# An RWKV7 mixer rearranged: decay on the state, key-query products among the projections, joined inverses in two wide tiles

## The chip, the cores and the metric

The kernel runs on one core of a Trainium2 chip. The metric is the device time of one execution in microseconds. The time before is 3166.21 us, the median of three runs (3164.11 to 3168.96).

TensorE (PE) does matmuls and transposes, VectorE (DVE) elementwise work and 32x32 block transposes, ScalarE (ACT) activations and copies, GpSimd (POOL) elementwise work and fills; the SyncE queue (SP) issues the loads of weights.

## The reference, cut to what matters

The program is a transformer of six layers in fp32. The last four are blocks of FFN, mixer, FFN; the mixer of the first and the last of these is an RWKV7 time mix (16 heads of 64, 256 tokens). It is this:

```
dx = token_shift(h) - h
xr, xw, xk, xv, xa, xg = [h + dx * mu[j] for j in range(6)]
r, k, v = xr @ w_rkv[0], xk @ w_rkv[1], xv @ w_rkv[2]
w = -softplus(-(w0 + tanh(xw @ w1) @ w2)) - 0.5
decay = exp(-exp(w))
a = sigmoid(a0 + (xa @ a1) @ a2)
if vres is None: v_first = v                 # first call
else: v = v + (v_first - v) * sigmoid(v0 + (xv @ v1) @ v2)   # second call
g = sigmoid(xg @ g1) @ g2
kk = normalized heads of k * k_k
k = k * (1 + (a - 1) * k_a)
def step(state, inp):                        # for each token, per head 64x64
    sa = state @ -kk_t
    state = state * w_t + outer(sa, kk_t * a_t) + outer(v_t, k_t)
    return state, state @ r_t
y = group norm of the outputs over each head, * ln_w + ln_b
bonus = sum(r * k * r_k) * v                 # per head and token
out = ((y + bonus) * g) @ w_o
```

## The kernel before, in words

One function, `rwkv(i, j)` (lines 1351 to 1778), does a whole mixer and is called twice: j = 0 near 883 to 1150 us of the profiled span, j = 1 near 2690 to 2945 us. Channels lie on partitions; a tile of 128x512 holds 128 channels twice by 256 tokens, so that the 1024 channels are four such tiles (index w) or eight halves (index k, two heads each). The tokens are cut into four chunks (index c) of 64. Within a chunk the recurrence becomes matrix products and the inverse of a unit triangular 64x64 matrix per head and chunk; between the chunks a state is carried.

A weight matrix of 128x2048 comes from memory into one of three staging slots ("raw", line 334 on); ScalarE rounds it to a high part wH (L341), VectorE subtracts to make the low part wL (L343), and TensorE multiplies with high and low parts (function `mm3`; L320 is the line of every plain matmul). The names of the stages below are mine.

- **A, preparation.** For each w the projection of r runs, and `prep(w)` forms the normalized keys kk, the cumulated decay W and its inverse iW (a scan cs and two exponentials), kw (keys times decay, L1492, and a copy of its first columns, L1493), and the tiles AP and BK. BK holds two halves: L1504 on VectorE, L1505 on GpSimd, which also clears AP. `inter(w)` multiplies AP with BK on TensorE (phb), transposes AP (phe), and leaves masked triangles in L3 (tile lc) and AM.
- **B, inverse by columns.** VectorE transposes L3 in four pieces (L1614), then subtracts column after column in 31 steps (L1621, L1623) and transposes the result twice (L1626 and L1627, tile tdt). Two inverses of 32x32 stand for each 64x64 triangle. Between the column steps `late()` issues other work in portions: the mixes and low-rank products for g and v (l1b, l1c), the v projection, in the second call the gate sv and the mixing of v with the first layer's v (vf, L1406 to L1408), and the second low-rank product of g (matmuls ps<-g,raw).
- **C, `reads()`.** For each w: the product r times k times r_k (L1575) summed by a matmul (bs), r times decay (L1577), the key-query products pha of TensorE with 64 rows, their masks PA (L1586), bh = BK times the decay at a chunk's end (L1591, half on GpSimd), its transposes pt, kept as BKT, and the bonus tiles.
- **D, joining.** The 32x32 inverses become 64x64 ones: products pn and px of 32x32 matrices, copies into block tiles BD (64 on ScalarE, 32 on VectorE, each 32x128), and GT = AM times BD (matmul pg).
- **E, the chunks.** For each c: `values` (pv), `solve` (pu, then two copies into sv), `advance` (matmul pst with BKT, the new state), `read` (py), the norm, and `back`. The state is pst plus ws, the old state times the decay, which GpSimd makes (L1717).

The order of the work is not the order of the code alone: a scheduler of the framework places the instructions on each engine by priority, and tiles wait for free slots of their pools: three raw slots, three "big" ones, 44 data tiles of 128x512 ("d"), three PSUM tiles "ps", two for transposes, two "otile".

Of the kernel before, what the change touches and what calls it, by code (L numbers as in the profile page):

```python
# [241 lines left out]
class Kern:  # L242
# [1108 lines left out]
    def rwkv(self, i, j):  # L1351
        nc, A = self.nc, self.A
        vres = j > 0
        rb = self.rstd_b()
# [121 lines left out]
        def prep(w):  # L1476
# [17 lines left out]
            for m in range(2):  # L1494
# [10 lines left out]
                nc.gpsimd.tensor_tensor(b4[:, :, 64:128], c4(kt[w], m), c4(iW, m), OP.mult)  # L1505
# [19 lines left out]

        next(rproj)
        prep(0)
        for w in range(4):
            if w < 3:
                prep(w + 1)  # L1530
                next(rproj)
            inter(w)
        GG = BO = None
# [34 lines left out]
        def reads():  # L1568

            for w in range(4):  # L1570
                pb = self.otile("bs")
                for m in range(2):
                    k, sl = 2 * w + m, slice(m * 256, m * 256 + 256)
                    q = self.t2("rk")[:, :256]
                    nc.vector.scalar_tensor_tensor(q, r[w][:, sl], vj("r_k", k), kt[w][:, sl], op0=OP.mult, op1=OP.mult)  # L1575
                    self.mm(pb[:, sl], self.cc("bd"), q)
                nc.vector.tensor_tensor(r[w], r[w], Wd[w], OP.mult)  # L1577
                pa_ = self.ps("pha"), self.ps("pha")
                for m in range(2):
                    for c in range(4):  # L1580
                        for hh in range(2):
                            rows = slice(hh * 64, hh * 64 + 64)
                            self.mm(pa_[hh][:, m * 256 + c * 64:m * 256 + c * 64 + 64], BK[2 * w + m][rows, c * 128:c * 128 + 128], c4(r[w], m)[rows, c])
                for hh in range(2):
                    pa = self.d("PA")
                    nc.vector.scalar_tensor_tensor(y3(pa), self.cc("lt").unsqueeze(1).to_broadcast([128, 8, 64]), 0.0, y3(pa_[hh]), op0=OP.is_equal, op1=OP.mult)  # L1586
                    PA.append(pa)
                for m in range(2):
                    k, bk = 2 * w + m, BK[2 * w + m]
                    bh = self.d("bh")  # L1590
                    (nc.vector if m else nc.gpsimd).tensor_tensor(x4(bh), x4(bk), c4(Wd[w], m)[:, :, 63:64].to_broadcast([128, 4, 128]), OP.mult)  # L1591
                    pt = self.ptile()
                    for c in range(4):
# [5 lines left out]
                bo, gg = (t[:, w * 512:w * 512 + 512] for t in (BO, GG))  # L1599
                nc.vector.tensor_tensor(bo, pb, v[w], OP.mult)  # L1600
                for m in range(2):
                    k = 2 * w + m
                    sl = slice(m * 256, m * 256 + 256)
                    nc.vector.scalar_tensor_tensor(bo[:, sl], bo[:, sl], vj("ln_b", k), gg[:, sl], op0=OP.add, op1=OP.mult)
                    nc.scalar.activation(gg[:, sl], gg[:, sl], AF.Copy, scale=vj("ln_w", k))

        BKT, PA = [], []
# [24 lines left out]
        GT = []  # L1632
# [458 lines left out]
```

## Time and profile before

| | |
|---|---|
| median of three runs | 3166.21 us |
| profiled execution | 3169.24 us |
| its span | 3167.1 us |
| mean granted clock | 0.95 |
| TensorE, VectorE, ScalarE, GpSimd busy | 93%, 76%, 52%, 5% |

The profile is one execution taken by the hardware profiler. The granted clock is the share of TensorE's full 2.4 GHz that it had in a stretch; its lower level is 1.2 GHz. Ends of matmuls are modelled, so the distance of starts tells more than a matmul's length. The stages are cut at these moments of the span, in us: first call A 965.5, B 1008.2, C 1057.4, D 1088.25, E 1122.9 to 1149.9; second call A 2748.0, B 2794.4, C 2856.0, D 2883.0, E 2917.6.

### The profile page before, as it was taken

Reading aid. Unit: us, or ns where it says so; the run is one execution under the profiler, and the core shown is the slowest. Engines: PE = TensorE matmul, PEld = TensorE weight load, DVE = VectorE, ACT = ScalarE, POOL = GpSimd, SP = SyncE. Lnnn points to the kernel's source line nnn. Section 1 sums busy time; section 2 is a strip of 40 time slices with the busy share of each in tenths; the row PEclk is TensorE's granted clock in tenths of the full one; section 3 lists DMA queues with packets and bytes.
Section 4 is the critical chain, followed back from the end, with each engine's and each line's share of the span. In section 5 each row is a group of like instructions: output and inputs, shape, how many; then the busy total and the mean of one; then the engine's idle time right before and its main releaser. Section 6 shows DMA issues by size and latency. Waiting matters only on the chain.

```text
span 3167.1 us, 58978 instructions
## 1 busy us (share of the span) xinstructions
PE 2949.1 (93%) x22797; PEld 2656.4 (84%) x22797; DVE 2404.6 (76%) x5855; ACT 1635.9 (52%) x3593; POOL 160.4 (5%) x259
## 2 busy tenths in 40 slices
PE   8888888889988989999999999999899999889999
PEld 7665666579976889999898899998699998678898
DVE  6863686378769668888798789887789887795765
ACT  4551445155556355555578655554555554635554
POOL 0000000010001110000000000000000000001000
PEclk9898989899989799999999999999999999888999
DMA  7538874986643237776643577767367866331543
GB/s 278 198 139 340 307 261 143 370 303 238 218 155 119 94 136 256 261 281 232 248 175 145 173 248 277 287 225 281 109 240 273 298 241 244 104 100 55 173 165 116
DMA packets 117964, 673.45 MB, mean 213 GB/s; under 512 B 13392, under 2 KB 14288, under 8 KB 56112
## 3 DMA queue, kind: packets, MB, share of 16 engines
q1 hardware_dynamic: 112016, 659.23, 58.4%
q10 hardware_dynamic: 5664, 10.41, 1.0%
q8 instruction: 181, 2.97, 0.4%
q14 instruction: 103, 0.84, 0.1%
HBM read 667.49 MB, written 2.10 MB: 211 GB/s over the span
## 4 chain that ended last, share of the span: by engine, by line
PE 73%; DVE 10%; ACT 3%; issue 1%; DMA 1%; POOL 0%; ACTq 0%; DVEq 0%; SPq 0%
PE ps L320 27%; PE pa L320 16%; PE pb L320 16%; DVE wL L343 2%; PE mo L320 1%; ACT wH L341 1%; DVE raw L1320 1%; PE pg L320 1%; PE pha L320 1%; PE pe L320 1%; DMA raw<-in_rkv 1%; PE st L320 1%; PE xg L320 1%; PE sc L320 1%; PE pv L320 1%
## 5 line engine op out<-in xcount | busy, mean ns | idle before, releaser
L341 ACT ACTIVATE wH<-raw 128x512 fp32r<-128x512 f32 (+1 forms) x1656 | 855.3, 577 | 548.3 <-PE ps L320 216.9
L343 DVE TENSOR_TENSOR wL<-raw,wH 128x512 fp32r<-128x512 f32 (+4 forms) x1048 | 942.5, 917 | 113.3 <-ACT wH L341 103.8
L1320 DVE CUSTOM_DVE_ANT_0 raw<-raw,cb 128x512 f32<-128x512 f32 x576 | 378.6, 694 | 57.3 <-DMA raw<-in_adaw 57.1
L320 PE MATMUL pb<-xnH,wH 128*128 128x258 f32 x1408 | 348.5, 285 | 4.9 <-ACT xnH L484 4.9
L320 PE MATMUL pb<-xnL,wH 128*128 128x258 f32 x1408 | 347.6, 283 | 0.0
L320 PE MATMUL ps<-g,wH 128*128 128x512 f32 x1408 | 347.4, 394 | 0.0
L320 PE MATMUL pa<-xnH,wH 128*128 128x258 f32 x1408 | 347.4, 284 | 0.0
L320 PE MATMUL pa<-xnL,wH 128*128 128x258 f32 x1408 | 347.1, 284 | 0.0
L320 PEld LDWEIGHTS ps<-g,wH 128*128 128x128 f32 x1408 | 256.1, 188 | 50.9
L320 PEld LDWEIGHTS pb<-xnH,wH 128*128 128x128 f32 x1408 | 266.6, 190 | 5.5 <-ACT xnH L484 5.1
L320 PEld LDWEIGHTS pa<-xnL,wH 128*128 128x128 f32 x1408 | 268.4, 191 | 0.0
L320 PEld LDWEIGHTS pa<-xnH,wH 128*128 128x128 f32 x1408 | 268.1, 190 | 0.0
L320 PEld LDWEIGHTS pb<-xnL,wH 128*128 128x128 f32 x1408 | 267.4, 190 | 0.0
L416 ACT ACTIVATE g<-fh 128x256 fp32r<-128x256 f32 x176 | 73.7, 418 | 257.3 <-DVE fh L2001 257.2
L320 PE MATMUL pa<-xnH,wL 128*128 128x258 f32 x1408 | 199.0, 284 | 0.0
L320 PE MATMUL pb<-xnH,wL 128*128 128x258 f32 x1408 | 199.0, 284 | 0.0
L320 PEld LDWEIGHTS ps<-g,wL 128*128 128x128 f32 x1408 | 184.8, 189 | 11.0
L320 PE MATMUL ps<-g,wL 128*128 128x256 f32 x1408 | 187.8, 281 | 0.0
L320 PEld LDWEIGHTS pb<-xnH,wL 128*128 128x128 f32 x1408 | 182.6, 191 | 0.0
L320 PEld LDWEIGHTS pa<-xnH,wL 128*128 128x128 f32 x1408 | 182.2, 190 | 0.0
L433 POOL TENSOR_TENSOR ssum<-ssum,sq 128x256 f32<-128x256 f32 x95 | 80.4, 847 | 1902.5 <-ACT sq L431 1717.2
L320 PE MATMUL ps<-nH,wH 128*128 128x256 f32 (+1 forms) x456 | 115.3, 291 | 3.3 <-ACT nH L518 3.3
(574 smaller groups left out, 5840.4 us busy)
## 6 DMA issues: line engine op xcount, KB each, us to landing
raw<-in_fin SPq DMA_DIRECT2D x176, 1024.0 KB, 5.0
raw<-in_adaw SPq DMA_DIRECT2D x144, 1024.0 KB, 5.1
raw<-in_fout SPq DMA_DIRECT2D x128, 704.0 KB, 4.6
mw<-in_mgu SPq DMA_DIRECT2D x48, 1024.0 KB, 8.9
mw<-in_mdn SPq DMA_DIRECT2D x28, 1024.0 KB, 11.4
raw<-in_rkv SPq DMA_DIRECT2D x24, 1024.0 KB, 5.0
raw<-in_mbi SPq DMA_DIRECT2D x24, 1024.0 KB, 4.9
mp<-in_mgu SPq DMA_DIRECT2D x64, 256.0 KB, 6.7
```

The source lines that it names most:

```text
L320: self.nc.tensor.matmul(out, lhsT, rhs, start=start, stop=stop)
L341: self.nc.scalar.activation(H[:, a:b], r[:, a:b], AF.Copy)
L343: self.nc.vector.tensor_tensor(L[:, a:b], r[:, a:b], H[:, a:b], OP.subtract)
L416: self.nc.scalar.activation(dst[0], src, AF.Copy)
L433: nc.gpsimd.tensor_tensor(self.ssum, self.ssum, sq, OP.add)
L1320: self.nc.vector.tensor_tensor_reduce(wm, wm, self.cb[:, h * 512:h * 512 + 512], 1.0, 0.0, OP.mult, OP.add, self.raws[i][:, h, 2 * b + m:2 ...
```

## The change

Six edits, all inside `rwkv`. (1) The low parts of its weights are made in two pieces of 1024 columns instead of four of 512. (2) The second half of BK is made by VectorE. (3) `reads` runs within the loop of A, once for each w, and no longer scales the keys: it transposes BK itself; r_k times r times k overwrites k; the bonus matmuls become `bonus(w)`, called after `values(0)`. (4) The transposes of L3 are one of 128 partitions and two of 32. (5) The block tiles of the joining are two of 128x2048, one from the raw slots (cleared after the transposes of L3 in the code), one from the big ones; copies into them are 32 partitions by 16 blocks, and pn and px alternate between the two row groups at every matmul. (6) The state is scaled as a whole: it is pst times the decay WC on VectorE, and the old state enters pst through a matmul with the identity.

```diff
+        cutl, self.cutl = self.cutl, 2
...
-                nc.gpsimd.tensor_tensor(b4[:, :, 64:128], c4(kt[w], m), c4(iW, m), OP.mult)
+                nc.vector.tensor_tensor(b4[:, :, 64:128], c4(kt[w], m), c4(iW, m), OP.mult)
...
+        def reads(w):
+            for m in range(2):
+                k, sl = 2 * w + m, slice(m * 256, m * 256 + 256)
+                pt = self.ptile()
+                for c in range(4):
+                    nc.tensor.transpose(pt[:, c * 128:c * 128 + 128], BK[k][:, c * 128:c * 128 + 128], self.ident)
+                bt = self.d("BKT")
+                nc.scalar.activation(bt, pt, AF.Copy)
+                BKT.append(bt)
+                nc.vector.scalar_tensor_tensor(kt[w][:, sl], r[w][:, sl], vj("r_k", k), kt[w][:, sl], op0=OP.mult, op1=OP.mult)
+            nc.vector.tensor_tensor(r[w], r[w], Wd[w], OP.mult)
+            pa_ = self.ps("pha"), self.ps("pha")
+            for m in range(2):
+                for c in range(4):
+                    for hh in range(2):
+                        rows = slice(hh * 64, hh * 64 + 64)
+                        self.mm(pa_[hh][:, m * 256 + c * 64:m * 256 + c * 64 + 64], BK[2 * w + m][rows, c * 128:c * 128 + 128], c4(r[w], m)[rows, c])
+            for hh in range(2):
+                pa = self.d("PA")
+                nc.vector.scalar_tensor_tensor(y3(pa), self.cc("lt").unsqueeze(1).to_broadcast([128, 8, 64]), 0.0, y3(pa_[hh]), op0=OP.is_equal, op1=OP.mult)
+                PA.append(pa)
+        BKT, PA = [], []
...
+            reads(w)
...
-                    k, bk = 2 * w + m, BK[2 * w + m]
-                    bh = self.d("bh")
-                    (nc.vector if m else nc.gpsimd).tensor_tensor(x4(bh), x4(bk), c4(Wd[w], m)[:, :, 63:64].to_broadcast([128, 4, 128]), OP.mult)
-                    pt = self.ptile()
-                    for c in range(4):
-                        nc.tensor.transpose(pt[:, c * 128:c * 128 + 128], bh[:, c * 128:c * 128 + 128], self.ident)
-                    bt = self.d("BKT")
-                    nc.scalar.activation(bt, pt, AF.Copy)
-                    BKT.append(bt)
-                    yield
...
+        def bonus(w):
+            pb = self.otile("bs")
+            for m in range(2):
+                sl = slice(m * 256, m * 256 + 256)
+                self.mm(pb[:, sl], self.cc("bd"), kt[w][:, sl])
+            bo, gg = (t[:, w * 512:w * 512 + 512] for t in (BO, GG))
+            nc.vector.tensor_tensor(bo, pb, v[w], OP.mult)
...
-        for q in range(4):
-            rows = slice(32 * q, 32 * q + 32)
-            c0 = (q % 2) * 32
+        for rows, c0 in ((slice(0, 128), 0), (slice(32, 64), 32), (slice(96, 128), 32)):
             nc.vector.transpose(Lp[rows], L3[rows, :, c0:c0 + 32].rearrange("p m j -> p j m"))
+        bd = [self.rawp.tile([128, 2048], FT, name="bd", tag="raw")]
+        nc.gpsimd.memset(bd[0], 0.0)
...
+        bd.append(self.big("bd"))
+        nc.gpsimd.memset(bd[1], 0.0)
...
+        two = (nc.vector.tensor_copy, lambda o, i: nc.scalar.activation(o, i, AF.Copy))
+        fs = [(slice(64 * hh, 64 * hh + 32), slice(64 * hh + 32, 64 * hh + 64)) for hh in range(2)]
+        bd = [t.rearrange("p (m x) -> p m x", m=16) for t in bd]
+        nts, GT = [], []
         for half in range(2):
-            pn, px = self.ps("pn"), self.ps("px")
-            nt = self.t2("nt")
+            pn, nt = self.ps("pn"), self.t2("nt")
+            for m in range(16):
+                for f, s2 in fs:
+                    self.mm(pn[f, m * 32:m * 32 + 32], L3[s2, 16 * half + m, 0:32], Td[s2, 16 * half + m])
             for hh in range(2):
-                f, s2 = slice(64 * hh, 64 * hh + 32), slice(64 * hh + 32, 64 * hh + 64)
-                for m in range(16):
-                    mm_ = 16 * half + m
-                    self.mm(pn[f, m * 32:m * 32 + 32], L3[s2, mm_, 0:32], Td[s2, mm_])
-                nc.vector.tensor_copy(nt[f], pn[f])
-                for m in range(16):
-                    mm_ = 16 * half + m
-                    self.mm(px[f, m * 32:m * 32 + 32], Tn[f, mm_], nt[f, m * 32:m * 32 + 32])
-            bds = []
+                two[hh](nt[fs[hh][0]], pn[fs[hh][0]])
+            nts.append(nt)
+        for half in range(2):
+            h16 = slice(16 * half, 16 * half + 16)
+            for q in range(4):
+                rows = slice(32 * q, 32 * q + 32)
+                two[q // 2](bd[half][rows, :, 32 * q:32 * q + 32], Td[rows, h16])
+            px = self.ps("px")
+            for m in range(16):
+                for f, s2 in fs:
+                    self.mm(px[f, m * 32:m * 32 + 32], Tn[f, 16 * half + m], nts[half][f, m * 32:m * 32 + 32])
+            for hh in range(2):
+                f = fs[hh][0]
+                two[hh](bd[half][f, :, 64 * hh + 32:64 * hh + 64], px[f].rearrange("p (m x) -> p m x", m=16))
             for kq in range(4):
                 k = 4 * half + kq
-                b = self.d("BD")
-                nc.gpsimd.memset(b, 0.0)
-                b4 = x4(b)
-                for q in range(4):
-                    rows = slice(32 * q, 32 * q + 32)
-                    nc.scalar.activation(b4[rows, :, 32 * q:32 * q + 32], Td[rows, 4 * k:4 * k + 4], AF.Copy)
-                for hh in range(2):
-                    f = slice(64 * hh, 64 * hh + 32)
-                    nc.vector.tensor_copy(b4[f, :, 64 * hh + 32:64 * hh + 64], px[f, kq * 128:kq * 128 + 128].rearrange("p (c x) -> p c x", c=4))
-                bds.append(b)
-            for kq in range(4):
-                k, b = 4 * half + kq, bds[kq]
                 pg = self.otile("pg")
                 for c in range(4):
-                    self.mm(pg[:, c * 128:c * 128 + 128], AM[k][:, c * 128:c * 128 + 128], b[:, c * 128:c * 128 + 128])
+                    self.mm(pg[:, c * 128:c * 128 + 128], AM[k][:, c * 128:c * 128 + 128], bd[half][:, 4 * kq + c])
...
-                pn, ws = state
                 S = self.d("SP")
-                if ws is None:
-                    nc.vector.tensor_copy(S, pn)
-                else:
-                    nc.vector.tensor_tensor(S, pn, ws, OP.add)
+                nc.vector.tensor_tensor(y3(S), y3(state[0]), bc(WC[:, c - 1]), OP.mult)
                 nc.scalar.activation(s4[:, :, 0], y3(S[0:64]), AF.Copy)
...
-            ws = None
+            pn = self.ps("pst")
             if c:
-                ws = self.d("ws")
-                nc.gpsimd.tensor_tensor(y3(ws), y3(SP[c]), bc(WC[:, c]), OP.mult)
-            pn = self.ps("pst")
+                self.mm(pn, self.ident, SP[c], True, False)
             for k in range(8):
                 for hh in range(2):
                     self.mm(pn[hh * 64:hh * 64 + 64, k * 64:k * 64 + 64], BKT[k][:, c * 128 + hh * 64:c * 128 + hh * 64 + 64],
-                            SV[:, k * 128 + hh * 64:k * 128 + hh * 64 + 64])
-            state[:] = pn, ws
+                            SV[:, k * 128 + hh * 64:k * 128 + hh * 64 + 64], c == 0, c == 0 or k == 7)
+            state[:] = [pn]
 
...
         values(0)
+        for w in range(4):
+            bonus(w)
...
+        self.cutl = cutl
```

The scheduler places all this anew. On TensorE in stage A of the first call, around the first `inter`, before (ps<-rxH is the r projection, phb and phe belong to `inter`):

```order
L320 MATMUL ps<-rxH,wH 128x256
L320 MATMUL ps<-rxL,wH 128x256
L320 MATMUL ps<-rxH,wL 128x256 x8
L320 MATMUL phb<-BK,AP 128x128
...
L320 MATMUL phb<-BK,AP 128x128
L1516 MATMUL phe<-cst,AP 128x128
L320 MATMUL kn<-rn,sel 128x256 x2
L320 MATMUL ps<-rxH,wH 128x256
```

and in the changed kernel (pt are the transposes of BK, pha the key-query products):

```order
L320 MATMUL ps<-rxH,wL 128x256 x4
L1533 MATMUL pt<-cst,BK 128x128 x3
L320 MATMUL phb<-BK,AP 128x128
L1517 MATMUL phe<-cst,AP 128x128
...
L1517 MATMUL phe<-cst,AP 128x128
L1533 MATMUL pt<-cst,BK 128x128 x5
L320 MATMUL ps<-rxH,wL 128x256 x4
...
L320 MATMUL ps<-rxL,wH 128x256
L320 MATMUL ps<-rxH,wL 128x256 x8
L320 MATMUL pha<-r,BK 128x64 x16
L320 MATMUL kn<-rn,sel 128x256 x2
L320 MATMUL ps<-rxH,wH 128x256
```

The transposes surround `inter`, and a block of 16 products stands behind the next half of the projection. On TensorE at the end of the g products of the first call, before (bs are bonus matmuls):

```order
L320 MATMUL ps<-g_10901,raw 128x256
L320 MATMUL bs<-rk,cst 128x256 x2
L320 MATMUL pha<-r,BK 128x64 x16
L320 MATMUL bs<-rk,cst 128x256 x2
...
L320 MATMUL pha<-r,BK 128x64
L320 MATMUL pn<-tdt,lc 32x32 x16
...
L320 MATMUL pn<-tdt,lc 32x32 x30
L320 MATMUL px<-nt,tdt 32x32 x16
L320 MATMUL pn<-tdt,lc 32x32 x2
L320 MATMUL pv<-cst,v 64x128 x8
L320 MATMUL pg<-BD,AM 128x128 x12
```

and in the changed kernel:

```order
L320 MATMUL ps<-g_11042,raw 128x256
L320 MATMUL pn<-tdt,lc 32x32 x64
L320 MATMUL px<-nt,tdt 32x32
L320 MATMUL pv<-cst,v 64x128
L320 MATMUL px<-nt,tdt 32x32 x63
L320 MATMUL pv<-cst,v 64x128 x7
L320 MATMUL pg<-bd,AM 128x128 x8
...
L320 MATMUL pg<-bd,AM 128x128 x8
L320 MATMUL bs<-k,cst 128x256 x6
L320 MATMUL pu<-sv,GT 64x64 x11
L320 MATMUL pv<-cst,v 64x128 x8
L320 MATMUL bs<-k,cst 128x256 x2
```

The 64 pn matmuls follow g, px stands nearly in one run, and the bonus matmuls moved behind pg, among the first solve matmuls pu and the v matmuls pv. A little later, in the second chunk's solve, the identity matmul pst<-SP,cst stands behind the first pu:

```order
L320 MATMUL pu<-sv,GT 64x64
L320 MATMUL pst<-SP,cst 128x512
L320 MATMUL pu<-sv,GT 64x64 x15
L320 MATMUL py<-Z,r 64x128
L320 MATMUL pst<-sv,BKT 64x64
```

It is queued ahead of the other 15 pu and of the state matmuls pst<-sv,BKT. On VectorE in the second call, at the end of the column loop, before (vf and v are the mixing of v):

```order
L1621 TENSOR_TENSOR ru<-lpt 128x31
L1575 SCALAR_TENSOR_TENSOR rk<-r,vec,k 128x256
L1623 TENSOR_TENSOR lpt<-lpt,ru 128x31
L1575 SCALAR_TENSOR_TENSOR rk<-r,vec,k 128x256
L1626 STREAM_TRANSPOSE tdt<-lpt 128x32x32
L1627 STREAM_TRANSPOSE tdt<-lpt 128x32x32
L1577 TENSOR_TENSOR r<-r,sg 128x512
L1406 TENSOR_TENSOR vf<-vf,ps 128x512
L1575 SCALAR_TENSOR_TENSOR rk<-r,vec,k 128x256
L1407 TENSOR_TENSOR vf<-vf,sv 128x512
L1575 SCALAR_TENSOR_TENSOR rk<-r,vec,k 128x256
L1408 TENSOR_TENSOR v<-ps,vf 128x512
```

and in the changed kernel:

```order
L1622 TENSOR_TENSOR lpt<-lpt,ru 128x31
L1625 STREAM_TRANSPOSE tdt<-lpt 128x32x32
L1407 TENSOR_TENSOR vf<-vf,ps 128x512
L1626 STREAM_TRANSPOSE tdt<-lpt 128x32x32
L1408 TENSOR_TENSOR vf<-vf,sv 128x512
L343 TENSOR_TENSOR wL<-raw,wH 128x1024 x2
L1647 COPY bd<-tdt 32x16x32 x4
L343 TENSOR_TENSOR wL<-raw,wH 128x1024
L1407 TENSOR_TENSOR vf<-vf,ps 128x512
L343 TENSOR_TENSOR wL<-raw,wH 128x1024
L1408 TENSOR_TENSOR vf<-vf,sv 128x512
L1409 TENSOR_TENSOR v<-ps,vf 128x512 x3
```

The low parts of two tiles of v weights (four pieces wL) and the mixing of several v tiles now stand behind the first or second of the transposes tdt, where before only the last tile's mixing did.

## Rows read from the trace of the kernel before

**Rows 1.** Stages A to E, first call; A to D, second: us, PE, PEld, DVE, ACT, POOL, clock

```profile
965.50:1008.20 42.70, 38.43 (x287) 35.84 (x286) 41.66 (x85) 33.36 (x70) 10.75 (x16) 0.96 0.35 118
1008.20:1057.40 49.20, 42.03 (x255) 33.97 (x254) 46.52 (x102) 15.65 (x31) 1.66 (x2) 0.90 0.25 86
1057.40:1088.25 30.85, 27.20 (x169) 21.55 (x168) 19.66 (x33) 7.03 (x14) 5.39 (x8) 0.63 0.18 69
1088.25:1122.90 34.65, 32.86 (x429) 30.40 (x428) 12.90 (x33) 20.25 (x51) 3.96 (x8) 0.78 0.19 63
1122.90:1149.90 27.00, 18.75 (x380) 16.59 (x380) 18.85 (x41) 16.76 (x41) 3.80 (x10) 0.96 0.36 119
2748.00:2794.40 46.40, 40.86 (x292) 38.06 (x290) 41.79 (x82) 31.55 (x67) 10.65 (x16) 0.93 0.20 66
2794.40:2856.00 61.60, 45.36 (x286) 36.68 (x285) 59.23 (x123) 17.48 (x35) 2.96 (x3) 0.89 0.28 93
2856.00:2883.00 27.00, 25.14 (x165) 21.09 (x163) 18.27 (x40) 8.54 (x17) 4.40 (x6) 0.72 0.30 117
2883.00:2917.60 34.60, 33.49 (x433) 30.76 (x433) 10.46 (x25) 20.80 (x51) 3.96 (x8) 0.77 0.10 32
```

**Rows 2.** Timeline of TensorE, first call, end of B and C: start, us, instruction

```profile
1050.36 7.07 PE L320 MATMUL ps<-g,raw 128*128 128x256 f32 x32
1057.26 1.03 PE L320 MATMUL bs<-rk,cst 128*128 128x256 f32 x4
1058.22 2.00 PE L320 MATMUL pha<-r,BK 64*128 64x64 f32 x32
...
1065.33 0.44 PE L320 MATMUL pha<-r,BK 64*128 64x64 f32 x4 [3.40 <-DVE PA L1586]
...
1075.69 1.97 PE L320 MATMUL pha<-r,BK 64*128 64x64 f32 x16
```

**Rows 3.** Tiles kk, BK, rk, PA, lpt: duration ns min/median/max, first and last start

```profile
L1492 DVE TENSOR_TENSOR kw<-kk,sg x8: 671/1219/1231, 972.1 to 2784.8; 128x504 f32<-128x504 f32 x8
L1493 DVE COPY kw<-kk x8: 164/954/1192, 973.3 to 2785.9; 128x8 f32<-128x8 f32 x8
...
L1505 POOL TENSOR_TENSOR BK<-k,iW x16: 714/952/1064, 971.8 to 2786.2; 128x256 f32<-128x256 f32 x16
L1504 DVE TENSOR_TENSOR BK<-a,iW x16: 411/414/958, 973.9 to 2786.4; 128x256 f32<-128x256 f32 x16
...
L1575 DVE SCALAR_TENSOR_TENSOR rk<-r,vec,k x16: 469/477/3892, 1050.9 to 2860.3; 128x256 f32<-128x256 f32 x16
...
L1586 DVE SCALAR_TENSOR_TENSOR PA<-cst,pha x16: 675/682/689, 1064.6 to 2883.1; 128x512 f32<-128x512 f32 x16
...
L1614 DVE STREAM_TRANSPOSE lpt<-lc x8: 1884/1894/1940, 1008.2 to 2800.2; 32x1024 f32<-32x1024 f32 x8
```

**Rows 4.** Timeline of TensorE, first call, stage D

```profile
1093.88 0.24 PE L320 MATMUL px<-nt,tdt 32*32 32x32 f32 x1
...
1094.02 2.88 PE L320 MATMUL pn<-tdt,lc 32*32 32x32 f32 x54
...
1107.85 1.08 PE L320 MATMUL pn<-tdt,lc 32*32 32x32 f32 x29
...
1117.09 2.05 PE L320 MATMUL pg<-BD,AM 128*128 128x128 f32 x16
```

**Rows 5.** Timeline of VectorE, second call, end of stage B

```profile
2836.30 0.68 DVE L1406 TENSOR_TENSOR vf<-vf,ps 128x512 f32<-128x512 f32 x1
...
2847.20 2.03 DVE L1627 STREAM_TRANSPOSE tdt<-lpt 128x1024 f32<-128x1024 f32 x1
```

**Rows 6.** Page, costliest groups (busy, mean ns, idle) and DMA issues (KB, us)

```profile
L1320 DVE CUSTOM_DVE_ANT_0 raw<-raw,cb 128x512 f32<-128x512 f32 x576 | 378.6, 694 | 57.3 <-DMA raw<-in_adaw 57.1
...
raw<-in_rkv SPq DMA_DIRECT2D x24, 1024.0 KB, 5.0
```

**Rows 7.** Timeline of TensorE, first call, stage E

```profile
1128.20 0.33 PE L320 MATMUL pst<-sv,BKT 128*64 128x64 f32 x2 [1.33 <-ACT sv L1709]
```

More of the change, by code (lines that the diff above doesn't have):

```diff
@@ L1566, in late @@
                     nc.scalar.dma_start(self.vfd[w], v[w])
[L1568 to L1579, printed above, removed]
-                    for c in range(4):
-                        for hh in range(2):
[L1582 to L1588, printed above, removed]
-                    k, bk = 2 * w + m, BK[2 * w + m]
-                    bh = self.d("bh")
-                    (nc.vector if m else nc.gpsimd).tensor_tensor(x4(bh), x4(bk), c4(Wd[w], m)[:, :, 63:64].to_broadcast([128, 4, 128]), OP.mult)
-                    pt = self.ptile()
-                    for c in range(4):
-                        nc.tensor.transpose(pt[:, c * 128:c * 128 + 128], bh[:, c * 128:c * 128 + 128], self.ident)
-                    bt = self.d("BKT")
-                    nc.scalar.activation(bt, pt, AF.Copy)
-                    BKT.append(bt)
-                    yield
[L1599 to L1605, printed above, removed]
@@ L1607, in rwkv @@
-        BKT, PA = [], []
+        def bonus(w):
[5 more added lines that the diff above has]
+            nc.vector.tensor_tensor(bo, pb, v[w], OP.mult)
+            for m in range(2):
+                k = 2 * w + m
+                sl = slice(m * 256, m * 256 + 256)
+                nc.vector.scalar_tensor_tensor(bo[:, sl], bo[:, sl], vj("ln_b", k), gg[:, sl], op0=OP.add, op1=OP.mult)
+                nc.scalar.activation(gg[:, sl], gg[:, sl], AF.Copy, scale=vj("ln_w", k))
@@ L1627, in rwkv @@
         nc.vector.transpose(Tn.rearrange("p m c -> p c m"), Tp.rearrange("p i c -> p c i"))
+        bd.append(self.big("bd"))
+        nc.gpsimd.memset(bd[1], 0.0)
         for _ in lt:
             pass
-        for _ in reads():
-            pass
-        GT = []
+        two = (nc.vector.tensor_copy, lambda o, i: nc.scalar.activation(o, i, AF.Copy))
+        fs = [(slice(64 * hh, 64 * hh + 32), slice(64 * hh + 32, 64 * hh + 64)) for hh in range(2)]
+        bd = [t.rearrange("p (m x) -> p m x", m=16) for t in bd]
@@ L1646, in rwkv @@
             for kq in range(4):
                 k = 4 * half + kq
-                b = self.d("BD")
-                nc.gpsimd.memset(b, 0.0)
-                b4 = x4(b)
-                for q in range(4):
-                    rows = slice(32 * q, 32 * q + 32)
-                    nc.scalar.activation(b4[rows, :, 32 * q:32 * q + 32], Td[rows, 4 * k:4 * k + 4], AF.Copy)
-                for hh in range(2):
-                    f = slice(64 * hh, 64 * hh + 32)
-                    nc.vector.tensor_copy(b4[f, :, 64 * hh + 32:64 * hh + 64], px[f, kq * 128:kq * 128 + 128].rearrange("p (c x) -> p c x", c=4))
@@ L1668, in rwkv @@
         Y, O = [], []
-        SU, SP, state = {}, {}, [None, None]
+        SU, SP, state = {}, {}, [None]
         Z = [[self.d("Z") for _ in range(2)] for _ in range(2)]
```

## Prediction

> **What bounds the kernel now.** I read the page first: TensorE is busy 93% of the span, so only the two calls of the recurrent mixer that the change touches need a close look. I cut each call by the instruction that starts a stage: A, preparation beside the r projection; B, from the transposes of L to the last g matmul; C, the reads stage (bonus, key-query products, transposes of keys); D, joining of the inverses, up to the first state matmul; E, the four chunks. The table by stage [rows 1] is the backbone. In A, VectorE is busy 41.66 of 42.70 us and TensorE 38.43: both nearly full. In B of the first call (VectorE 46.5 of 49.2, TensorE 42.0) TensorE waits some 7 us at the start, while VectorE transposes L. In C and D TensorE is nearly always busy and VectorE is not, but the granted clock is 0.63 and 0.78: much of the time goes at 1.2 GHz. Rows of one stage show both levels: the 64-row products take 2.00 us for 32 rows at 1058.22, then TensorE waits 3.40 us for VectorE, and afterwards 16 such rows take 1.97 us [rows 2]. An fp32 matmul leaves two rows, a transpose one. E is a chain of small steps through all engines, half idle.
>
> **Stage A: what comes in.** Per call VectorE gets 16 multiplies of keys by r and r_k (0.48, L1575), 8 masks of the products (0.68, L1586) [rows 3] and 4 multiplies of r by the decay, of the masks' size and so taken at 0.68 too; from row to row VectorE's pipelined starts lie about 0.08 closer than these durations, so 8 x 0.40 + 4 x 0.60 + 8 x 0.60 = 10.4 us (eight of the sixteen rows belong to each call; the listed counts are for both). The last two masks fall behind the transposes, so 9. The second halves of BK come over from GpSimd: 8 x 0.34 (L1504, the same operation, runs beside them) = 2.7. Against this: while GpSimd runs its BK multiplies, VectorE's kw takes a median 1.22 us against 0.67 at best, and the tiny copy behind it 0.95 against 0.16 [rows 3]; with GpSimd's multiplies gone I take 4 x (0.55 + 0.75) = 5.2 off (bounds 0 and 6). The first scan now stands ahead of a wait of VectorE's before A, 1.2 off. Sum for VectorE: 9 + 2.7 - 5.2 - 1.2 = +5. Two conversions of 1024 columns in place of four of 512 change nothing but a few pipeline gaps.
>
> The rule on ports, GPSIMD Engine Reference of the Trainium skill (Specifications), says that GpSimd's SBUF interfaces are shared with VectorE and contend with VectorE instructions that have two SBUF inputs or use two ports. The kw rows agree for the multiply; a copy of eight columns at 0.95 goes further than I would have read from it. By rule alone the two-input kw would give 2.2 us a call, by the rows 5.2.
>
> TensorE gets 64 product matmuls, 128 rows x 0.0625 = 8 us at full clock [rows 2], and 32 transposes, 32 rows x 0.13 (as pg's rows of the same size, 16 in 2.05 [rows 4]) = 4. So TensorE's A goes from 38.4 to about 50, of which the last group's 3 fall into B's wait. VectorE near 47, TensorE near 47, each waiting for the other at times: A about +8 (first call) and +6 (second, which had 4.6 us of VectorE waits). Bounds: 0, all of it in gaps and in B's opening wait; +16, VectorE's 12 and some waits between the two.
>
> Every added product block switches TensorE between 128-row and 64-row shapes. The Trainium skill, TensorEngine Tiling (Array Packing), Key Properties, says that changing the tiling mode drains TensorE, a rule against this change. Here four bonus rows ahead of a product block take 0.96 to the block's start, 0.24 a row, against 6.90 / 32 = 0.22 within a run of the same size [rows 2]: a drain is 0.1 us at most, so 16 more switches a call cost under 1.6 us by the rows; the sum leaves it out.
>
> **Stages B and C, first call.** One of four transposes of L goes: -1.9 (L1614) [rows 3], on the path because TensorE waits there. A 128-partition transpose I take to cost as a 32-partition one, as the later 128x1024 one does (2.03 [rows 5]). C as a stage disappears, 30.85 us: the products and transposes went to A, and the bonus matmuls go to D. The joining follows the last g matmul directly. -33 (bounds -33, -25).
>
> **Second call.** One zeroed block matrix now holds one of the three staging slots from A on, and products and transposed keys fill the data tiles early. The loads of the v weights go one after another through one slot, 5.0 us each [rows 6] plus the two conversions (about 3 us), and VectorE's order puts the conversions and evacuations of v2 and v3 behind the last transpose, where before they stood in the column loop. The loop gets shorter: before, the last transpose ended at 2849.2, 54.8 into B [rows 5]. Three evacuations of v (three instructions of 0.60: 2836.30 is the first of one [rows 5]) and some 3 us of conversions and rk leave it, and one transpose of L, so it ends near 44. From there v2 and v3 (5.7 us of matmuls each), their evacuations and g (32 rows x 0.22 = 7) with their waits take about 23: the joining starts at 67 to 69 in place of 61.6 + 27.0 = 88.6 [rows 1]. -20 (bounds -33 as in the first call, and -12).
>
> **Stage D.** TensorE's 32.86 us at clock 0.78 are 25.6 at full clock. Out: two groups of four transposes, 1.1. In: 16 bonus rows, 3.8. The pn and px rows: within one kind and one row group 54 take 2.88, 0.053 a row, at half clock; at full, 29 take 1.08, 0.037; but where pn and px alternate, the six starts from 1093.88 to 1094.02 lie 0.028 apart, also at half clock [rows 4]. The new order alternates row groups at every matmul, so 256 rows x 0.035 = 9 could become 4.5. I take that half as good as half: -2. That is 26.3, plus waits: pg for the copy of px, and the bonus, since VectorE's copy of the first solved values now stands behind the fourth bonus multiply; 2.5. At full clock 28.8 against 34.65: -6. The 64 copies on ScalarE (20.25 us busy) become a few wide ones, but they were not what TensorE waited for at the end. Bounds: -11 with the pairs fully beside each other, +9 if the clock stays at about 0.7.
>
> The same skill page, same section, says that different tiles run matmuls in parallel; the alternating rows agree. By the rule in full, D would be 2.5 us shorter still in each call.
>
> **Stage E.** The state's decay becomes VectorE's multiply in place of an add or copy of the same 0.69; GpSimd's product was off the path. New is the identity matmul of 128x512: two rows of twice 0.22, 0.9 us, twice a call, after the first of the chunk's solve matmuls. Behind it wait the other 15, then both copies of the solved values, then the state matmuls. At one of the two places ScalarE was later anyway (state matmul waited 1.33 for it [rows 7]). +1. In the first call four L1320 instructions (0.69 [rows 6]) now stand among E's steps on VectorE, +2; v matmuls ahead of the first state matmul, +1. So +4 and +2 (bounds 0 and +7).
>
> **Sum.** First call +8 - 33 - 6 + 4 = -27; second +6 - 20 - 6 + 2 = -18. Together -45: the profiled execution's 3169.2 becomes 3124; the median of the runs shown is 3 lower than that execution, so 3121. I say 3121, with 3108 to 3135 as this case's own range.
>
> **Rivals.**
> 1. The prep hides everything: products and transposes go into gaps and B's opening wait (A +0, 14 off), the second call gains as the first (13 off), pairs run beside each other (5 off). 3121 - 32 = 3089, or some part of it: 3095 to 3107. For it: TensorE idles 7 us at the start of B in the first call and 16 in all in B of the second [rows 1]. Against: A has both engines at 90% and over.
> 2. The gain is smaller: the reads' work reappears in A at its whole TensorE price (27.2 us x 0.63 = 17 a call instead of 8 and 6: +20), or the second call's slots hold the v projection so that its 18 go. 3139 to 3141. For it: the single slot and VectorE's order. Against: about 20 us stand between even that and the old start of the joining.
> 3. Slower: TensorE's clock. The 64-row and 32-row matmuls that now stand in A and at the start of D, with waits between, could bring what rows 2 show after 1065: 1.2 GHz. Work at half clock takes twice as long, so the gain of 45 is eaten once 45 us of A's and D's TensorE work (47 + 26 us a call at full clock, 146 in all) run so; with D wholly and a third of A at half clock, 3121 + 2 x (26 + 16) = 3205. For it: the clock of 0.63 in C, which held such work. Against: that fall followed a wait of 3.40, and the same rows ran at full clock before it; in A dense projection matmuls stand between.
> 4. It does not do what it says, the transposes of keys and products being bound by VectorE just as before, so that nothing moves: only if A grows by 45.
>
> **Chances.** Forecast 0.52; rival 1, 0.19; rival 2, 0.22; rival 3, 0.04; rival 4 or mixtures near no change, 0.03. The range 3099 to 3146 holds the forecast, rival 2 and half of rival 1. What a measurement of this kernel tells from no change is about 0.2%, 6 us: faster 0.93, same 0.03, slower 0.04.
>
> **What would show it.** In the trace of the changed kernel: A of 48 to 54 us with kw at 0.67 and the copy at 0.16; no stage between the last g matmul and pn in the first call; in the second pn some 20 us earlier after the transposes begin, with v2's matmuls after the last transpose; a joining near 29 at a clock over 0.9 with pn rows 0.02 to 0.035 apart; in E a period 0 to 1 us longer. Wrong it would be if A is over 60, if the clock in D stays below 0.8, or if the second call's joining starts 80 us after B begins.

## The result, and the profile after

The changed kernel takes 3131.8 us (median of five runs, 3126.4 to 3135.1); the kernel before took 3164.1 in the same comparison. The ratio is 0.9889, 95% interval 0.9872 to 0.9906: 32 us faster by the medians, 35 by the ratio. Forecast were 3121 and 45 us, with a range of 3099 to 3146.

The profiled execution has a span of 3129.9 against 3167.1, 37 us less, but not all of that is the change's. The first mixer begins (issue of the identity's load) at 871.2 us against 882.8, behind instructions that stand in the same order. Over fourteen profiles of this study this moment lies anywhere between 868.5 and 882.8, and a second profile of the kernel before has 875.0. So the comparison goes stage by stage inside the two calls. The windows of the changed kernel, cut at the same instructions as [rows 1] (us, then busy PE, PEld, DVE, ACT, POOL, granted clock, DMA share, GB/s): A, B, D of the first call, then of the second.

```profile
955.70:1004.50 48.80, 45.23 (x383) 42.81 (x384) 45.60 (x96) 32.22 (x70) 3.86 (x5) 0.93 0.17 57
1004.50:1053.87 49.37, 43.95 (x292) 35.02 (x290) 47.23 (x98) 17.43 (x34) 2.13 (x2) 0.93 0.26 87
1053.87:1086.05 32.18, 29.60 (x438) 26.10 (x439) 11.57 (x22) 19.15 (x35) 3.16 (x6) 0.84 0.27 99
2715.20:2771.09 55.89, 51.16 (x417) 47.99 (x417) 46.77 (x98) 32.49 (x69) 3.85 (x5) 0.91 0.07 25
2771.09:2848.97 77.88, 56.67 (x324) 44.47 (x322) 57.57 (x115) 22.99 (x45) 2.12 (x2) 0.82 0.25 82
2848.97:2879.82 30.85, 27.39 (x431) 24.11 (x431) 13.36 (x31) 16.48 (x31) 3.04 (x5) 0.89 0.39 138
```

C is gone in both calls: B and C together fell from 80.05 to 49.37 in the first and from 88.60 to 77.88 in the second. A grew by 6.1 and 9.5, D fell by 2.5 and 3.7. From the identity's load to the last output tile the first call is 23.6 us shorter, the second 4.9 (8.5 against the second profile of the kernel before).

Against [rows 3], the tile kk of the changed kernel shows VectorE's multiply kw and the copy behind it without GpSimd beside them (duration min/median/max in ns):

```profile
L1493 DVE TENSOR_TENSOR kw<-kk,sg x8: 674/676/678, 960.0 to 2758.7; 128x504 f32<-128x504 f32 x8
L1494 DVE COPY kw<-kk x8: 166/168/171, 960.6 to 2759.3; 128x8 f32<-128x8 f32 x8
```

Against [rows 4], TensorE's timeline at the start of D in the first call of the changed kernel (start, length, operation, tiles, rows, and in brackets the wait ahead of it):

```profile
1053.87 1.20 PE L320 MATMUL pn<-tdt,lc 32*32 32x32 f32 x64
1055.95 1.10 PE L320 MATMUL pn<-tdt,lc 32*32 32x32 f32 x58 [0.88 <-ACT wH L1426]
...
1057.55 1.54 PE L320 MATMUL px<-nt,tdt 32*32 32x32 f32 x49
1060.65 2.24 PE L320 MATMUL px<-nt,tdt 32*32 32x32 f32 x77 [1.56 <-issue]
```

The pn rows lie 0.016 to 0.017 apart (58 rows from 1055.95 to 1056.87), less than half of the 0.037 in [rows 4]. The px rows lie 0.027 apart ahead of the 1.56 us in which TensorE stands for nothing that the profile names (49 rows, the last of them at 1058.85), and 0.028 behind it. Both are at half clock: the granted clock is 1.00 up to 1057.28 and 0.50 from there to 1067.52. The window of the half clock:

```profile
1057.28:1067.52 10.24, 8.68 (x149) 7.93 (x148) 1.96 (x3) 3.50 (x6) 0.94 (x1) 0.50 0.30 122
```

So the pairs run beside each other as hoped, and the clock takes part of it back: 0.84 in this D. It fell ahead of the 1.56 us, not because of them.

In the second call the gate sv is the thing to see. Eight instructions of ScalarE write it, two for each of its four tiles. From ScalarE's timeline in the changed kernel, the fourth, fifth and seventh of them, and what stands ahead of the last two:

```profile
2797.23 0.47 ACT L1424 ACTIVATE sv<-ps,vec 128x256 f32<-128x256 f32 x1 [0.38 <-PE ps L320]
...
2806.12 0.63 ACT L341 ACTIVATE wH<-raw 128x512 fp32r<-128x512 f32 x1 [6.34 <-DMA raw<-in_rkv]
2806.72 0.47 ACT L1424 ACTIVATE sv<-ps,vec 128x256 f32<-128x256 f32 x1
...
2816.49 0.63 ACT L1631 ACTIVATE bd<-tdt 32x512 f32<-32x512 f32 x1 [7.38 <-DVE tdt L1625]
...
2819.54 0.47 ACT L1424 ACTIVATE sv<-ps,vec 128x256 f32<-128x256 f32 x1 [0.21 <-DVE vf L1408]
```

The first two tiles are written by 2797.7, the third from 2806.7 and the fourth from 2819.5. The third stands in ScalarE's order behind a conversion that waits 6.34 us for weights; the fourth stands behind a copy that waits 7.38 us for the transposed inverses, and then waits 0.21 us for the data tile that VectorE releases (vf L1408). So the trace by itself does not tell whether the staging slot or the data tiles put these writes so late; e1 and e2 below decide it. TensorE waits for these writes (its timeline):

```profile
2807.24 0.70 PE L320 MATMUL ps<-g,raw 128*128 128x256 f32 x2 [2.48 <-ACT sv L1424]
...
2820.06 1.22 PE L320 MATMUL ps<-g,raw 128*128 128x256 f32 x2 [4.08 <-ACT sv L1424]
```

Later it waits 3.33 us, up to 2834.68, for VectorE's evacuation of v (L1409).

### The profile page after: what moved, and what is told of

Read it like the earlier page. It is cut to its first block, busy times and chain, and to the rows that moved or that the text cites. A ratio compares the mean times of both kernels' runs of the same rounds, so it can differ in the third digit from the quotient of the medians.

```text
span 3129.9 us, 58786 instructions
## 1 busy us (share of the span) xinstructions
PE 2915.6 (93%) x22805; PEld 2621.8 (84%) x22805; DVE 2380.1 (76%) x5789; ACT 1624.8 (52%) x3545; POOL 130.9 (4%) x219
## 4 chain that ended last, share of the span: by engine, by line
PE 66%; DVE 7%; ACT 3%; DMA 2%; issue 1%; POOL 0%; ACTq 0%; DVEq 0%; SPq 0%
PE ps L320 25%; PE pa L320 16%; PE pb L320 16%; DVE wL L343 1%; PE mo L320 1%; DMA raw<-in_adaw 1%; ACT wH L341 1%; PE pg L320 1%; PE py L320 1%; DVE raw L1320 1%; DMA raw<-in_rkv 0%; PE st L320 0%; PE pv L320 0%; DVE ru L1620 0%; DVE lpt L1622 0%
## 5 line engine op out<-in xcount | busy, mean ns | idle before, releaser
L343 DVE TENSOR_TENSOR wL<-raw,wH 128x1024 fp32r<-128x1024 f32 (+3 forms) x1000 | 938.2, 954 | 114.1 <-ACT wH L341 105.1
L433 POOL TENSOR_TENSOR ssum<-ssum,sq 128x256 f32<-128x256 f32 x95 | 78.2, 823 | 1891.8 <-ACT sq L431 1550.1
```

The lines of the kernel that those rows point to most:

```text
L343: self.nc.vector.tensor_tensor(L[:, a:b], r[:, a:b], H[:, a:b], OP.subtract)
L433: nc.gpsimd.tensor_tensor(self.ssum, self.ssum, sq, OP.add)
```

## The experiments

All but the fourth start from the changed kernel. One table for all, from the first starts in each trace: A from the reciprocal of the key norms to the first transpose of L; BC from there to the first pn; D to the first state multiply on VectorE; E to the last output tile; call from the identity's load to that tile. First call / second call, in us. Each ratio is to the kernel before as timed in the same comparison.

| run | median us | ratio (95%) | A | BC | D | E | call |
|---|---|---|---|---|---|---|---|
| before | 3164.1 | | 44.6/45.0 | 80.0/88.6 | 35.9/35.9 | 26.3/24.7 | 267.6/263.8 |
| changed | 3131.8 | 0.9889 (0.9872 to 0.9906) | 50.6/54.5 | 49.4/77.9 | 33.4/32.1 | 27.9/26.0 | 244.0/258.9 |
| e1 | 3129.5 | 0.9899 (0.9867 to 0.9931) | 51.3/54.5 | 48.8/76.0 | 32.5/31.7 | 27.5/25.6 | 241.5/256.6 |
| e2 | 3120.5 | 0.9858 (0.9818 to 0.9899) | 52.3/55.7 | 50.6/60.4 | 32.7/31.8 | 27.5/26.1 | 244.6/244.5 |
| e3 | 3113.6 | 0.9851 (0.9808 to 0.9894) | 51.0/55.9 | 48.8/60.0 | 32.5/31.6 | 27.5/25.8 | 241.0/243.3 |
| e4 | 3164.4 | 1.0004 (0.9984 to 1.0024) | 46.1/45.4 | 80.0/92.0 | 35.8/35.6 | 26.3/24.7 | 267.4/267.4 |
| e5 | 3124.2 | 0.9858 (0.9823 to 0.9892) | 43.4/43.9 | 70.4/72.3 | 28.3/26.4 | 29.4/27.6 | 253.5/240.5 |
| e6 | 3134.2 | 0.9895 (0.9849 to 0.9942) | 51.0/54.7 | 49.6/77.9 | 35.1/33.4 | 27.5/25.6 | 245.6/260.3 |
| e7 | 3144.8 | 0.9934 (0.9906 to 0.9961) | 51.0/51.5 | 49.6/77.4 | 32.3/32.0 | 29.9/31.0 | 243.9/261.6 |
| e8 | 3135.2 | 0.9898 (0.9867 to 0.9929) | 53.5/53.7 | 49.8/77.5 | 32.5/32.2 | 27.4/26.1 | 244.1/259.1 |
| e9 | 3127.5 | 0.9882 (0.9861 to 0.9902) | 56.2/56.7 | 50.6/61.2 | 33.8/32.2 | 28.0/26.1 | 246.8/243.9 |
| e10 | 3118.7 | 0.9855 (0.9833 to 0.9878) | 57.8/45.4 | 51.3/75.5 | 32.5/24.6 | 27.5/27.1 | 247.3/241.7 |
| e11 | 3130.2 | 0.9891 (0.9870 to 0.9913) | 57.7/56.6 | 51.2/61.3 | 32.7/32.3 | 27.5/26.1 | 247.5/243.5 |
| e12 | 3116.9 | 0.9851 (0.9832 to 0.9870) | 53.9/44.4 | 49.4/72.4 | 32.8/26.4 | 27.5/27.1 | 244.7/238.2 |

**e1, e2, e3: what holds the second call.** e1 takes the first block tile from the staging slots after the projections:

```diff
-        bd = [self.rawp.tile([128, 2048], FT, name="bd", tag="raw")]
-        nc.gpsimd.memset(bd[0], 0.0)
         lt = late()
...
         for _ in lt:
             pass
+        bd = [self.rawp.tile([128, 2048], FT, name="bd", tag="raw"), bd1]
+        nc.gpsimd.memset(bd[0], 0.0)
```

Here `bd1` is the second block tile, taken from the big ones as before.

> The changed kernel, but the first wide block tile is taken from the staging slots only after the v and g projections, so that all three slots serve the v weights. In the changed kernel the second call takes 133.8 us from its first scan to the first pn matmul (2715.2 to 2849.0). Theory 1, the staging slot holds the v weights back: that stretch falls by 12 us or more, to under 122, and the time from 3132 to about 3118. Theory 2, the 44 data tiles are full and hold the gate sv and the evacuation of v back: the stretch falls by under 5 us, time 3127 to 3132, and VectorE still mixes the last v tiles behind the last transpose.

e2 uses six data tiles fewer in the second call:

```diff
-                o = self.d(name)
+                o = sv[w] if name == "v" and vres else self.d(name)
...
-                o = self.d(name) if dst is None else dst[:, w * 512:w * 512 + 512]
+                o = (self.t2(name) if name == "sv" and w == 3 else self.d(name)) if dst is None else dst[:, w * 512:w * 512 + 512]
...
-            g1, g2 = self.d("g1")[:, :256], self.d("g2")[:, :256]
+            g1 = self.d("g1")
+            g1, g2 = g1[:, :256], g1[:, 256:512]
```

> The changed kernel with six data tiles fewer in use in the second call: v is written over the gate sv, g1 and g2 share one tile, the last sv lies in the small temporary pool. The staging slots are as in the changed kernel. Theory 2 (full data tiles): from the first scan to the first pn 133.8 falls to under 120, time about 3116. Theory 1 (staging slot): under 5 us, time 3127 to 3132, v matmuls still one tile at a time behind their loads.

e3 has both edits.

> Both edits of the two runs before. Theory 1: as the first run alone within 3 us. Theory 2: as the second alone within 3 us. If both hold the second call back, it is shorter than either alone by 4 us or more; then time about 3110.

The data tiles it is: BC of the second call falls by 17.5 us with e2, by 1.9 with e1, by 17.9 with both. From the first scan to the first pn, 133.8 becomes 117.6, 131.9 and 117.4. The six tiles come from three edits at once; which of them counts no run separates. In e2 ScalarE writes all of sv within 6.2 us (first and last of six rows with eight instructions):

```profile
2800.45 0.91 ACT L1424 ACTIVATE sv<-ps,vec 128x256 f32<-128x256 f32 x2 [1.49 <-PE ps L320]
...
2806.14 0.47 ACT L1424 ACTIVATE sv<-ps,vec 128x256 f32<-128x256 f32 x1
```

and in TensorE's timeline pn waits only for the transposed inverses:

```profile
2837.51 2.21 PE L320 MATMUL pn<-tdt,lc 32*32 32x32 f32 x128 [0.33 <-DVE tdt L1626]
```

**e4: the kernel before again.**

> The kernel before, unchanged, for a second profile. In the profile of before the first mixer begins at 882.8 us (issue of the identity load), in that of the changed kernel at 871.2, though the instructions ahead of it stand in the same order. If that is chance between executions, this profile begins anywhere from 868 to 888 and 882.8 was late; if it belongs to the changed program, it begins within 2 us of 882.8. Time 3154 to 3169 either way.

It began at 875.0: chance. Its calls take 267.4 and 267.4 against 267.6 and 263.8, so a call's time is told to about 4 us by one profile. The first call's is no better: e3 and e12 have the same first call, and it takes 241.0 and 244.7.

**e5: `reads(w)` after the last g product again,** the other edits kept.

```diff
             inter(w)
-            reads(w)
...
         for _ in lt:
             pass
+        for w in range(4):
+            reads(w)
```

> The changed kernel with the reads stage called after the last g product again, as in the kernel before; all other edits stay (no scaled keys, wide block tiles, state decay). My theory (TensorE runs the moved products and transposes in A at full clock and partly beside VectorE's work, so moving them removes a stage): in the first call A falls back from 48.8 to about 43, a stage of 18 to 25 us appears between the last g matmul and pn, and the first call is 15 us longer or more. Rival (the stage was long before because of the scaled keys and of half clock, and would now be short at either place): the new stage is under 10 us and the first call within 5 us of 3132's. In the second call fewer data tiles are full, so it gains there what e2 gained, up to 16 us; the total 3125 to 3150.

Between the two theories in the first call: with late reads it takes 253.5, 9.5 more than the changed kernel but 14 less than the kernel before. A is back at 43.4, the stage after g costs 20.4 us (1052.1 to 1072.5) instead of 31, and D falls to 28.3. That D has no better clock, 0.80 against 0.85 over the same stretch of the changed kernel; but TensorE's waits in it sum to 0.2 us instead of 2.4, and 22 rows of the v matmuls fewer stand in it, with E 1.5 us longer.

In the second call late reads are even better than early ones, 240.5 against 258.9. So as the changed kernel stands, calling the reads early wins 9.5 us in one call and loses 18.4 in the other; the whole of e5 (0.9858) is no slower than the changed kernel (0.9889), with intervals that overlap.

**e6: pn and px one row group after the other.**

```diff
-            for m in range(16):
-                for f, s2 in fs:
+            for f, s2 in fs:
+                for m in range(16):
```

> The changed kernel with pn and px issued one row group after the other, 16 matmuls each, instead of alternating. If alternating row groups let two 32x32 products run beside each other, the 128 rows of pn that take 2.2 us now take 4.4 (0.034 a row), px likewise, and D is 3 to 5 us longer in each call. If the pitch of 0.017 comes from anything else (a free weight path, the full clock), pn stays at 2.2 us and D within 1 us.

TensorE's timeline of e6 at the start of D:

```profile
1064.39 4.26 PE L320 MATMUL pn<-tdt,lc 32*32 32x32 f32 x125
1068.42 0.26 PE L320 MATMUL px<-nt,tdt 32*32 32x32 f32 x1
```

125 rows in 4.03 us, 0.032 each, twice the changed kernel's. D is 1.7 and 1.3 us longer, less than the 3 to 5 expected. Against e1, e2, e3 and e8, whose joining is the changed kernel's (32.5 to 32.7 in the first call, 31.6 to 32.2 in the second), it is 2.4 to 2.6 and 1.2 to 1.8; why not more is not shown. The granted clock falls here too, at 1068.12, though TensorE's timeline shows no wait from 1049.8 to there.

**e7: the bonus after the first state matmuls.**

```diff
         values(0)
-        for w in range(4):
-            bonus(w)
...
                 values(c + 1)
+            if c == 0:
+                for w in range(4):
+                    bonus(w)
```

> The changed kernel with the four bonus calls after the first chunk's solve and state matmuls instead of before its solve. In the changed kernel VectorE's copy of the first solved values starts at 1083.96 behind the fourth bonus multiply, 3.5 us after the last solve matmul. Theory (the bonus sits on the path between solve and state): from the first pn to the main run of state matmuls 32.2 falls to 28 or less, and the end of the mixer comes 2 to 4 us earlier in each call. Rival (the bonus only changes places with idle time later): the state matmuls start earlier but E grows by as much, since the state's multiply now stands behind the bonus.

The rival holds: D -1.1 and -0.1, and its 32.3 and 32.0 lie within 0.4 of runs that leave the bonus where it was (e1, e3: 32.5 and 31.6 to 31.7); E +2.0 and +5.0. The whole is no faster: 0.9934 against 0.9889, with intervals that just touch.

**e8: the second half of BK on GpSimd again** (L1506, `nc.gpsimd` for `nc.vector`).

> The changed kernel with the second half of BK back on GpSimd. Theory (GpSimd's multiplies cost VectorE more than they save it): kw goes from 0.68 back to 1.2 us in most of its eight runs and the copy behind it from 0.17 to 0.7 or more; VectorE's busy time in A of the first call goes from 45.6 to about 48, the stage is 0 to 3 us longer. Rival (VectorE is better off without the 16 multiplies): VectorE's busy time falls by 2.7 a call and A is shorter by 1 to 3 us.

The tile kk of e8:

```profile
L1493 DVE TENSOR_TENSOR kw<-kk,sg x8: 669/1212/1226, 962.6 to 2765.0; 128x504 f32<-128x504 f32 x8
L1494 DVE COPY kw<-kk x8: 161/948/1181, 963.7 to 2766.2; 128x8 f32<-128x8 f32 x8
```

The two durations rise as soon as GpSimd multiplies again. VectorE's busy time in A of the first call goes from 45.6 to 46.9 although eight multiplies left it, less than the 48 of the theory. For the stage it is undecided: A +2.9 in the first call, -0.8 in the second, and A moves by as much by chance (51.0 and 53.9 in e3 and e12, where TensorE, VectorE and ScalarE have the same order in it). The edit's worth is a few us at most.

**e9: the scan's mask loaded at the start of the mixer,** on top of e3.

```diff
         nc.scalar.dma_start(LT[:, 1024:], A["eye32"])
+        r64 = self.d("r64")
+        nc.scalar.dma_start(r64, A["r64"])
```

> The third run's kernel (block tile late, six data tiles fewer), and the scan's row of ones and zeros loaded at the start of each mixer instead of just ahead of its use. In the changed kernel VectorE waits 5.41 and 5.97 us for that load ahead of the first scan, and the norm of the keys, which stands behind the scan, waits too. Theory: the scan starts as soon as TensorE's sum or ScalarE's root is there, 3 to 5 us earlier in each call (the stretch from identity load to the reciprocal, 81.2 and 70.0, falls to 78 and 66); total about 3108. Rival: the wait goes over to the root, which comes only 2.7 us earlier, and the first call gains under 2, the second under 3.

VectorE's timeline, first call, changed kernel and then e9:

```profile
952.49 1.23 DVE L1487 TENSOR_TENSOR_SCAN cs<-r,sg 128x512 f32<-128x512 f32 x1 [5.41 <-DMA r<-in_r]
```

```profile
953.81 1.21 DVE L1487 TENSOR_TENSOR_SCAN cs<-r,sg 128x512 f32<-128x512 f32 x1
956.78 0.28 DVE L1467 TENSOR_SCALAR rn<-rn 16x256 f32<-16x256 f32 x1 [1.76 <-ACT rn L1466]
```

The wait went, and part of it came back as a wait for the root. Against e3, the stretch ahead of A fell from 81.2 to 78.2 in the first call as expected, and from 70.0 to 67.8 in the second, where 66 was expected. But the scheduler placed the work of A otherwise, and A of the first call rose from 51.0 to 56.2 (57.8 and 57.7 in e10 and e11, with the same order). Neither theory had that, and the 3108 did not come (3127.5); why A's new order is slower stays open.

**e10, e12: reads late in the second call alone,** on top of e9 and e3 (`vres` is set in the second call only).

```diff
-            reads(w)
+            if not vres:
+                reads(w)
...
+        if vres:
+            for w in range(4):
+                reads(w)
```

> The ninth run's kernel with the reads stage after the g products in the second call alone. With reads late everywhere (fifth run) the second call took 240.5 us from identity load to the last output tile, the first 253.5 against 244.0. Theory (in the second call the early products and transposed keys cost as much in data tiles, A and the joining as the stage saves): second call equal to or up to 4 us shorter than the ninth run's. Rival (the fifth run's second call was short only since its data tiles were free, which the ninth has by other means): the second call gets 8 us longer, as the first did.

> The third run's kernel (block tile late, six data tiles fewer) with the reads stage after the g products in the second call alone; the mask's load stays where the changed kernel has it. Theory (the calls add: the first is as in the third run, 241 us from identity load to last output tile, the second as in the fifth and tenth run, 240 to 242 against 243.3): total within 3 us of the third run's 3114, 16 to 22 us under the changed kernel's 3132. Rival (late reads in the second call cost 8 us there as in the first, with data tiles free): total 3120 or more.

The second call takes 241.7 and 238.2, against 243.9 and 243.3 with early reads: 2 and 5 us less, at the edge of what one profile tells, and not the rival's 8 more. With the data tiles free, A is 11 us shorter, BC 12 to 14 longer and D 5 to 8 shorter. e12 as a whole is no different from e3, whose first call happened to be 4 us shorter with the same edits there. Both stand at 0.9851 of the kernel before, the changed kernel at 0.9889: some 12 us less. That gain is barely clear of the noise: the interval of e12 ends at 0.9870, the changed kernel's begins at 0.9872, e3's overlaps it, and the three were timed in different comparisons.

**e11: nt in two tiles,** on top of e9: each engine copies its half of pn into a tile of its own (`nt = [self.t2("nt") for _ in range(2)]`).

> The ninth run's kernel with the two halves of nt (copies of pn on VectorE and ScalarE) in two tiles. In the changed kernel ScalarE's half starts only when VectorE's half has ended (1055.15 + 0.68, then after a wait for VectorE), though the rows are different. Theory (two engines that write one tile are put one after the other): the ScalarE copies start with VectorE's, px starts 0.6 us earlier for each half, D 1 to 2 us shorter per call. Rival (ScalarE was late for another reason): no change in D.

In the first call ScalarE's first copy starts at 1064.48, when ScalarE has ended other work (wH, 1063.38 + 1.08); the same holds in the changed kernel, so that copy shows nothing. The second still waits 0.91 us for VectorE's and starts at 1065.99, behind 1065.27 + 0.68. D stays within 1.1 us of e9's. The shared target is not the cause; the source, one PSUM tile read by both, remains as a guess.

## Why the prediction was right, and where it was not

Worked out from the table: the first call went from 267.6 to 244.0, -24 (forecast -27); the second from 263.8 or 267.4 to 258.9, -5 to -9 (forecast -18). Their sum, 29 to 32, is close to the 32 between the medians. The stated range allowed a gain of 20 to 67 us, so that falling inside it says little of the mechanism; the stages tell more.

- **A**, forecast +8 and +6, measured +6.0 and +9.5. The products and transposes came mostly at full clock and as priced (2.00 us for 32 rows of products, 0.97 for 8 transposes), and kw and the copy behind it fell to 0.68 and 0.17. In the first call both engines are near the 47 us of the sum (VectorE 45.6, TensorE 45.2); why the second call's A grew 3.5 us more than forecast is not shown. The early scan did not save the 1.2 us: in the first call it now waits 5.41 us for its mask's load, ahead of the norm. That sign was wrong; I had not asked when the mask's load lands. In the second call that wait was there before (6.25 us, now 5.97).
- **B and C, first call**: forecast -33, measured -30.7. e5 splits the whole first call: about 10 us come from having the reads early. The other 14 are there with late reads too: B and C 9.6 shorter, D 7.6, A 1.2, less 4.3 in E and ahead of A. Which of the other edits (no scaled keys, the bonus moved, one transpose fewer, the wide block tiles) gave how much, no run separates.
- **B and C, second call**: forecast -20, measured -10.7. This is the step that failed in size: the last transpose ended 47.9 us into B and not near 44, and the "about 23" us from there to the joining were 30.0. I had seen both the single staging slot and the full data tiles and took the slot as what counts; e1 and e2 show that the slot is worth 1.9 us, less than chance moves a call, and the tiles 17.5. With the tiles freed BC is 60.4, below my 67 to 69, since VectorE's order then puts the mixing of v back ahead of the transposes (the last of it ends at 2834.0, the first transpose starts at 2835.4).
- **D**, forecast -6, measured -2.5 and -3.7. The pairs run fully beside each other (0.017), and not half as I took it; against that the clock was 0.84 and 0.89, not full. By estimate from these, the first call's 28.8 less 2.5 for the pairs plus 0.16 x 32.2 = 5.1 for the clock is 31.4, of 32.2 measured. The trace of the kernel before already had the pitch at full clock: where px and pn alternate from 1107.73 to 1107.85, after the clock had risen at 1103.24, six steps take 0.12 us, 0.020 each; I had read only the place at half clock. My bound by a clock of 0.7 covered the fall, but that it follows a wait does not hold in general: here it fell behind a wait of 0.88, in e6 with no wait ahead of it. What makes it fall is open.
- **The waits in D** I put at 2.5 us, for the copy of px and the bonus. TensorE's waits there sum to 2.4 and 3.4 us, but they stand ahead of pn and px rows. Of the bonus e7 shows 1.1 and 0.1: taking it out of there gives nothing.
- **E**, forecast +4 and +2, measured +1.6 and +1.3.
- **Rivals.** Rival 1 had both engines of A at 90% and over; that held for the first call, in the second TensorE was at 88%. 1.2 GHz over A did not come: A ran at 0.93 and 0.91. Rival 2's second half had all 18 us of the second call lost to the staging slots; B and C lost 9.3 of their 20, and through the data tiles.
- **Signs.** A at 48.8 was in its 48 to 54, the second call's 55.9 above it. D at 32.2 and 30.9 was longer than 29, and its clock below 0.9. In the second call pn came 10.7 us earlier and not 20, at 77.9 us after B began; 80 would have counted as wrong.

## What to carry to other kernels

Work that is moved forward keeps its results alive for longer: count the buffers in use at the fullest moment before pricing the time, and look in the order for evacuations that slipped behind a long stretch. A stage that vanishes can be worth less than its length (here some 10 us of 31 in the first call); one run that puts the stage back and keeps the rest tells how much, and tells it for each call. Before a slow stretch is put down to the wait ahead of it, look at the rows ahead of that wait: here they were slow already. Compare stages between fixed instructions: the start of the first mixer, behind work that nobody touched, moved by up to 14 us between profiles, and by 7.8 between two of the same kernel.

## What the runs showed of the hardware

A VectorE copy of eight columns takes 0.17 us alone and 0.95 beside GpSimd's fp32 multiplies (medians; e8 turns it back), a two-input multiply of 504 columns 0.68 and 1.21. Rows of 32x32 products in two row groups start every 0.017 us at full clock when they alternate (0.027 at half clock) and every 0.032 when they do not (e6). A VectorE transpose of 128 partitions by 1024 columns takes 1.96 us, one of 32 partitions 1.89 to 1.97. The granted clock fell to half in e6 in the middle of pn rows, with no wait of TensorE in the 18 us before.
